# A two-block transformer kernel in split fp32: the closing layer norm moved to VectorE, and the last product's weights split during an earlier stage

## The chip, the cores and the metric

One core of one Trainium2 chip. The time is the device time of one execution in microseconds (us), median of three runs. The engines are called PE (TensorE), DVE (VectorE), ACT (ScalarE), POOL (GpSimd) and SP (SyncE, which issues the DMAs here).

## What is computed

Two blocks one after the other over 1024 tokens of width 1024, all in float32. The first has gated linear attention, a short convolution, a feed-forward part and a gated side input. The second has spatial gating, a convolution of 31 taps and attention in a window, whose three results are multiplied by `w_out_2`, added to the input and normed. The change touches the weights and the norm of the last two lines, and the feed-forward part's second product only as a place.

```python
h = h + (silu(a) * bb) @ w_down            # first block, feed-forward
...
def layer_norm(x, g, b):
    mu = jnp.mean(x, axis=-1, keepdims=True)
    var = jnp.mean(jnp.square(x - mu), axis=-1, keepdims=True)
    return (x - mu) * lax.rsqrt(var + 1e-5) * g + b
...
y = concatenate([ya, yb, yc], axis=-1) @ w_out_2      # second block
x = layer_norm(DEEPNORM_ALPHA * x + y, post_ln_g_2, post_ln_b_2)
```

## The kernel before

Every product runs on PE as three products of split operands: `split` (L308) makes a high part with an ACT copy (L313) and a low part with a DVE subtraction (L314), and `mm3` (L288) multiplies high by high, high by low and low by high (L293 to L295). Weights pass through one pool, `wts`: three raw tiles (raw0 to raw2), three of high and three of low parts; `load` (L85) fetches a tile, `split` (L104 ACT, L105 DVE) divides it.

The code is written as generators that are interleaved; a scheduler of the framework (`schedule_with_timeline_sim=True`) then fixes the order in which each engine gets its instructions. An engine works its queue in order, and SP issues all DMAs in order, so an instruction that waits holds up what is behind it on the same queue.

Three places matter here.

*The down projection* (`ffn_down`) multiplies the feed-forward's hidden values, which were spilled to DRAM as `sT`, by `w_down`. It runs in two parts of output columns; each part walks over pairs of hidden chunks. For each pair, `chunk` loads two pieces of `sT` (L987, tile sr) and splits them (tile s), one pair ahead of its 48 matmuls; a weight tile for the pair is loaded and split by the pool. This stage begins while the last of the up projection (`ffn_up`, L962 to L972) empties its banks.

*The attention units* of the second block (`run`): 16 units, one for each of 8 blocks of 128 tokens and 2 key heads. `att_scores` takes the scores (L1409 on PE, L1411 on DVE), the softmax (maximum L1414, exponentials L1418 and L1420 on ACT, sum L1421, reciprocal L1422, scaling L1426 on DVE and an ACT copy); `att_values` transposes, splits and multiplies by the values, and ends with L1455 (DVE) and L1456 (POOL) in the tile yc. During the first units `late_tiles` runs the last eight products of the block's input projection.

*The closing product.* With the fifth unit `finish_setup` loads the eight pieces of `w_out_2` (L1468, tile w2r) and splits each. Pieces 3 to 7 all use the raw tile raw0. From then on `finish(c)` runs for block c two blocks behind the attention: it loads the residual (L1489), splits ya and yb (low parts on POOL: mal) and yc, runs 48 matmuls (g), adds the residual on DVE (L1508), takes mean and variance (L1509, L1510), one over the root (L491 on DVE, L492 on POOL), and norms. For blocks 0 to 6 the norm is one small DVE product (L1513), an ACT pass (L1515: scale by the root's inverse, bias) and two POOL passes (L1516 by `post_ln_g_2`, L1517 plus `post_ln_b_2`); for block 7 it is two fused DVE instructions for each half of the columns (L1522, L1524). Then the result goes to DRAM (L1518, L1526).

Of the kernel before, what the change touches and what calls it, by code (L numbers as in the profile page):

```python
# [10 lines left out]
F32 = mybir.dt.float32  # L11
F32R = mybir.dt.float32r
U32 = mybir.dt.uint32
ACTF = mybir.ActivationFunctionType
ALU = mybir.AluOpType
# [4 lines left out]
D = 1024  # L20
# [115 lines left out]
class Kernel:  # L136
    def __init__(self, tc, ctx, I, out, dbg):
        self.tc, self.nc, self.ctx, self.I, self.out, self.dbg_out = tc, tc.nc, ctx, I, out, dbg or {}
        nc = self.nc
        self.cst = ctx.enter_context(tc.tile_pool(name="cst", bufs=1))  # L140
        self.wts = Weights(nc, ctx, tc, self.weight_plan())
        self.base = ctx.enter_context(tc.tile_pool(name="base", bufs=1))
        self.extra = None
        self.free_slots = {True: list(range(N_BASE)), False: []}
        self.slot_of = {}
        self.tmp = ctx.enter_context(tc.tile_pool(name="tmp", bufs=1))
        self.phase = None
        self.n_tmp = {}
        self.psum = self.banks = None
        self.dram = ctx.enter_context(tc.tile_pool(name="scr", bufs=1, space=DRAM))  # L150
        self.n_name = 0
        self.x_tiles = {}
        self.xT = self.dram.tile([2, 2, 128, 4, NH], F32, name="xT")
        self.hT = self.dram.tile([2, 2, 128, 4, NH], F32, name="hT")
        self.ppT = self.dram.tile([2, 128, 8, NH], F32, name="ppT")
        self.sT = self.dram.tile([NF, 128, 2, NH], F32, name="sT")


    def name(self, s):
# [818 lines left out]
    def ffn_down(self, N):  # L978

        nc, W = self.nc, self.wts  # L980
        kept = {}

        def chunk(k):
            if k in kept:
                return kept.pop(k)
            raw = self.temp([128, 2, NH], "sr", 2)
            nc.sync.dma_start(out=raw, in_=self.sT[k])  # L987
            s = self.slot([128, 4, NH], F32R, "s")
            self.split(s[:, 0:2, :], s[:, 2:4, :], raw)
            return s  # L990

        for hf in range(2):
            N[hf]["h"] = [self.slot([128, 4, NH], F32, "h", base=True) for _ in range(2)]
            for i in range(2):
                nc.sync.dma_start(out=N[hf]["h"][i], in_=self.hT[hf, i])
        self.stat = self.slot([128, 4, NH], F32, "stat", base=True)
        for hf in range(2):
            N[hf]["tiles"], N[hf]["act"] = [], []
        for part, pairs in enumerate(DOWN):
            ps = [self.psg("gx"[i // 4]) for i in range(8)]  # L1000
            nxt = [chunk(2 * pairs[0] + kk) for kk in range(2)]
            for n, j in enumerate(pairs):
                w = W.get("w_down", 256 * j, 2, part * 512, 512)
                s = nxt
                W.ahead()
                if n + 1 < len(pairs):
                    nxt = [chunk(2 * pairs[n + 1] + kk) for kk in range(2)]
                for half in range(2):
                    for kk in range(2):
                        for i in range(4 * half, 4 * half + 4):  # L1010
                            m, hf = divmod(i, 2)
                            wt = [x[:, kk, m * 128:(m + 1) * 128] for x in w]
                            self.mm3(ps[i], [(wt, (s[kk][:, hf, :], s[kk][:, 2 + hf, :]))],
                                     start=n == 0 and kk == 0, stop=n == len(pairs) - 1 and kk == 1)
                for kk in range(2):
                    if part == 0 and n >= len(pairs) - KEPT:
                        kept[2 * j + kk] = s[kk]
                    else:
                        self.release(s[kk])
            for hf in range(2):  # L1020
                tiles, act = self.alloc_act(4, True)
                N[hf]["tiles"] += tiles
                N[hf]["act"] += act
            for i in range(8):
                m, hf = divmod(i, 2)
                hm = N[hf]["h"][part][:, m, :]
                m += 4 * part
                nc.vector.tensor_tensor(out=hm, in0=ps[i], in1=hm, op=ALU.add)
                self.split(*N[hf]["act"][m], hm, self.v("ln3_g", m))
                self.square_acc(self.stat[:, hf, :], hm, m == 0)  # L1030
        for hf in range(2):
            N[hf]["r"] = self.norm_factor(hf, self.stat[:, hf, :])

    def load_pT(self):
        nc = self.nc
# [423 lines left out]
    def finish_setup(self):  # L1459
        nc, I = self.nc, self.I  # L1460
# [3 lines left out]
        nc.sync.dma_start(out=self.post[1], in_=I["post_ln_b_2"].to_broadcast([128, D]))  # L1464
        self.w2 = []
        for k in range(8):
            t = self.wts.pool.tile([128, D], F32, tag=f"raw{k if k < 3 else 0}", name=f"w2r{k}")
            nc.sync.dma_start(out=t, in_=I["w_out_2"][0, k * 128:(k + 1) * 128, :])  # L1468
            if k < 3:
                hi = self.wts.pool.tile([128, D], F32R, tag=f"hi{k}", name=f"w2h{k}")  # L1470
                lo = self.wts.pool.tile([128, D], F32R, tag=f"lo{k}", name=f"w2l{k}")
            elif k == 3:
                hi = self.wts.pool.tile([128, D], F32R, tag="raw1", name=f"w2h{k}")
                lo = self.wts.pool.tile([128, D], F32R, tag="raw2", name=f"w2l{k}")
            else:
                b = self.slot([128, 2, D], F32R, "w2")
                hi, lo = b[:, 0, :], b[:, 1, :]
            self.split(hi, lo, t)
            self.w2.append((hi, lo))

    def finish(self, c, ycs):

        nc = self.nc
        tok = slice(c * 128, (c + 1) * 128)
        if c % 2:
            res = self.wts.pool.tile([128, D], F32, tag="raw0", name=self.name("res"))
# [22 lines left out]
            nc.vector.bn_stats(out=st[:, 6 * n:6 * n + 6], in_=res[:, cl])  # L1509
        nc.vector.bn_aggr(out=st[:, 12:14], in_=st[:, 0:12])  # L1510
        self.small_rsqrt(st[:, 13:14], 1.0, 1e-5)
        if c < 7:
            nc.vector.tensor_scalar(out=st[:, 12:13], in0=st[:, 12:13], scalar1=st[:, 13:14], scalar2=-1.0, op0=ALU.mult,  # L1513
                                    op1=ALU.mult)
            nc.scalar.activation(out=res, in_=res, func=ACTF.Identity, scale=st[:, 13:14], bias=st[:, 12:13])  # L1515
            nc.gpsimd.tensor_tensor(out=res, in0=res, in1=self.post[0], op=ALU.mult)  # L1516
            nc.gpsimd.tensor_tensor(out=res, in0=res, in1=self.post[1], op=ALU.add)  # L1517
            nc.sync.dma_start(out=self.out[0, tok, :], in_=res)  # L1518
            return
        for n in range(2):  # L1520
            cl = slice(n * 512, (n + 1) * 512)
            nc.vector.scalar_tensor_tensor(out=res[:, cl], in0=res[:, cl], scalar=st[:, 12:13], in1=self.post[0][:, cl],  # L1522
                                           op0=ALU.subtract, op1=ALU.mult)
            nc.vector.scalar_tensor_tensor(out=res[:, cl], in0=res[:, cl], scalar=st[:, 13:14], in1=self.post[1][:, cl],  # L1524
# [119 lines left out]
```

## Time and profile before

| | |
|---|---|
| median of 3 runs | 1731.89 us (1731.1 to 1733.86) |
| profiled execution | 1733.28 us, its span 1731.5 us |
| PE clock granted, mean | 0.986 of full speed |
| PE busy | 1668.1 us (96% of the span) |
| DVE busy | 1135.5 us (66%) |
| ACT busy | 776.7 us (45%) |
| POOL busy | 377.6 us (22%) |
| DMA | 183.06 MB, mean 106 GB/s |

The busy times are of the whole span; the engines overlap, so they do not add up to it. The profile shows one execution on the hardware; the ends of matmuls in it are modelled. A line such as L1515 is a line of the kernel before. In the kernel after, lines behind L157 are higher by 1, those of `finish_setup` and what stands around it by 17 and less.

### The profile page before, as it was taken

The page shows a single profiled execution, that of the slowest core. Times are in us where ns is not written, and L with a number is a line of the kernel's source. Part 1 is how long each engine was busy: PE and PEld are TensorE (multiplying, and loading weights), DVE is VectorE, ACT ScalarE, POOL GpSimd, SP SyncE. Part 2 cuts the span into 40 slices and gives each one's busy share as a digit, 9 for nine tenths or more (in the row PEclk, how much of TensorE's full clock was granted, in tenths as well). Part 3 has the DMA queues.
Part 4 walks back from the last instruction along what each step waited for, and adds up shares of the span by engine and source line. Part 5 has one row for each costly group of instructions (what it writes and reads, how often), then busy time and mean ns, then how long its engine had stood idle before and what let it go on. Part 6 is the DMA issues. An engine that isn't in the chain of part 4 may idle for free.

```text
span 1731.5 us, 21021 instructions
## 1 busy us (share of the span) xinstructions
PE 1668.1 (96%) x7865; PEld 1380.5 (80%) x7865; DVE 1135.5 (66%) x1767; ACT 776.7 (45%) x1226; POOL 377.6 (22%) x307
## 2 busy tenths in 40 slices
PE   8999999999979999999999999999979999898997
PEld 6888987788758888888888888888858898786875
DVE  4256776987897556555644334329895998568786
ACT  5524246234555333333333223226577423578663
POOL 2010100200047444434420002003000000113664
PEclk9999999999999999999999999999989999999999
DMA  8233221324533222322236451434424412421111
GB/s 284 80 100 119 76 73 50 97 86 134 197 135 104 92 85 74 98 74 85 80 115 225 144 157 47 134 109 123 127 88 137 146 42 86 122 74 62 49 66 57
DMA packets 205022, 183.06 MB, mean 106 GB/s; under 512 B 8886, under 2 KB 173128, under 8 KB 203384
## 3 DMA queue, kind: packets, MB, share of 16 engines
q1 hardware_dynamic: 204920, 181.72, 33.4%
q8 instruction: 62, 1.02, 0.3%
q14 instruction: 40, 0.33, 0.1%
HBM read 149.17 MB, written 34.62 MB: 106 GB/s over the span
## 4 chain that ended last, share of the span: by engine, by line
PE 83%; DVE 9%; ACT 3%; issue 2%; DMA 2%; POOL 1%; SPq 0%; DVEq 0%; ACTq 0%; POOLq 0%
PE g L294 19%; PE g L295 19%; PE g L293 19%; PE x L293 6%; PE x L294 6%; PE x L295 6%; PE x L677 1%; DVE wl L105 1%; PE s L1409 1%; PE o L1447 1%; POOL sr L913 1%; PE t L1440 1%; PE x L639 1%; DVE stat L775 1%; DVE qpad L649 1%
## 5 line engine op out<-in xcount | busy, mean ns | idle before, releaser
L293 PE MATMUL g<-ah,wh 128*128 128x512 f32 x896 | 354.6, 399 | 11.4 <-issue 9.2
L294 PE MATMUL g<-al,wh 128*128 128x512 f32 x896 | 353.9, 396 | 0.4 <-DVE al L317 0.4
L295 PE MATMUL g<-ah,wl 128*128 128x512 f32 x896 | 353.8, 396 | 0.0
L104 ACT ACTIVATE wh<-wr 128x1024 fp32r<-128x1024 f32 (+1 forms) x142 | 150.2, 1061 | 267.3 <-PE g L294 170.1
L105 DVE TENSOR_TENSOR wl<-wr,wh 128x1024 fp32r<-128x1024 f32 (+1 forms) x142 | 181.1, 1278 | 117.6 <-ACT wh L104 113.8
L293 PEld LDWEIGHTS g<-ah,wh 128*128 128x128 f32 x896 | 169.7, 190 | 49.6 <-issue 11.6
L294 PEld LDWEIGHTS g<-al,wh 128*128 128x128 f32 x896 | 169.7, 189 | 37.9 <-issue 1.9
L295 PEld LDWEIGHTS g<-ah,wl 128*128 128x128 f32 x896 | 169.5, 189 | 37.3 <-issue 2.2
L314 DVE TENSOR_TENSOR s<-sr,s 128x1024 fp32r<-128x1024 f32 x36 | 44.0, 1222 | 99.9 <-ACT s L313 99.7
L913 POOL TENSOR_TENSOR sr<-wr,wr 128x512 f32<-128x512 f32 x22 | 46.5, 2112 | 180.2 <-DMA wr<-w_gate_upffn 143.0
L313 ACT ACTIVATE s<-sr 128x1024 fp32r<-128x1024 f32 x36 | 37.9, 1054 | 106.5 <-PE x L295 91.7
L958 POOL TENSOR_TENSOR t<-t,t 128x512 f32<-128x512 f32 x22 | 39.9, 1814 | 172.2 <-ACT t L941 172.2
L1299 DVE SCALAR_TENSOR_TENSOR cacc<-ypad,vec,cacc 128x1024 f32<-128x1024 f32 x60 | 76.1, 1292 | 0.4
L775 POOL TENSOR_TENSOR stat<-t,stat 128x512 f32<-128x512 f32 x14 | 23.5, 1703 | 234.6 <-ACT t L774 234.6
L293 PE MATMUL g<-s,wh 128*128 128x512 f32 x176 | 68.5, 389 | 0.0
L294 PE MATMUL g<-s,wh 128*128 128x512 f32 x176 | 68.5, 389 | 0.0
L295 PE MATMUL g<-s,wl 128*128 128x512 f32 x176 | 68.5, 389 | 0.0
L293 PE MATMUL x<-s,wh 128*128 128x512 f32 x176 | 68.5, 389 | 0.0
L294 PE MATMUL x<-s,wh 128*128 128x512 f32 x176 | 68.5, 389 | 0.0
L295 PE MATMUL x<-s,wl 128*128 128x512 f32 x176 | 68.5, 389 | 0.0
L649 DVE TENSOR_TENSOR qpad<-E,qk 64x64 f32<-64x64 f32 x224 | 51.2, 228 | 7.8 <-ACT E L641 5.0
L295 PE MATMUL g<-wh,al 128*128 128x256 f32 (+1 forms) x192 | 55.0, 288 | 0.0
(372 smaller groups left out, 3958.6 us busy)
## 6 DMA issues: line engine op xcount, KB each, us to landing
wr<-w_in SPq DMA_DIRECT2D x86, 512.0 KB
wr<-w_gate_upffn SPq DMA_DIRECT2D x44, 512.0 KB
sr<-sT SPq DMA_DIRECT2D x36, 512.0 KB
sT<-t SPq DMA_DIRECT2D x44, 256.0 KB
wr<-w_down SPq DMA_DIRECT2D x22, 512.0 KB
wr<-w_out SPq DMA_DIRECT2D x16, 512.0 KB
wr<-w_ple_gate SPq DMA_DIRECT2D x16, 512.0 KB
x<-x SPq DMA_DIRECT2D x8, 512.0 KB
```

What stands on the lines that cost most here:

```text
L104: self.nc.scalar.activation(out=hi[:, :n], in_=t[:, :n], func=ACTF.Copy)
L105: self.nc.vector.tensor_tensor(out=lo[:, :n], in0=t[:, :n], in1=hi[:, :n].bitcast(F32), op=ALU.subtract)
L293: mm(out=ps, lhsT=lh, rhs=rh, start=start and i == 0, stop=False)
L294: mm(out=ps, lhsT=lh, rhs=rl, start=False, stop=False)
L295: mm(out=ps, lhsT=ll, rhs=rh, start=False, stop=stop and i == n - 1)
L313: nc.scalar.activation(out=hi, in_=src, func=ACTF.Copy)
L314: (eng or nc.vector).tensor_tensor(out=lo, in0=src, in1=hi.bitcast(F32), op=ALU.subtract)
L649: nc.vector.tensor_tensor(out=qs[r, l, par, :].rearrange("p (b n) -> p b n", n=n), in0=right(E[r, 1 + l, :], n), in1=right(q[r], n), op=AL ...
L775: (eng or nc.gpsimd).tensor_tensor(out=acc, in0=sq, in1=acc, op=ALU.add)
L913: nc.gpsimd.tensor_tensor(out=t13[:, 0, :], in0=b12, in1=b11, op=ALU.subtract)
L958: nc.gpsimd.tensor_tensor(out=v5, in0=v5, in1=z7, op=ALU.add)
L1299: nc.vector.scalar_tensor_tensor(out=acc, in0=src, scalar=w, in1=acc, op0=ALU.mult, op1=ALU.add)
```

## The change

A DRAM tile `w2s` takes the split parts of `w_out_2`. A generator `split_w2` loads one piece of it into a tile w2r (two places), splits it into one of two tiles w2, and stores both parts; `ffn_down` takes one step of it in each pair of its first part, so eight steps in all. `finish_setup` no longer loads and splits: for each of the eight pieces it loads the two parts from `w2s`, 16 loads of 512 KB. In `finish` all blocks norm by the two fused DVE instructions: (res − mean) × `post_ln_g_2`, then × the root's inverse + `post_ln_b_2`; blocks 0 to 6 over the full width of 1024, block 7 in two halves as before. The ACT pass, the two POOL passes and the small DVE product are gone.

```diff
--- before.py
+++ after.py
@@ -154,6 +154,7 @@
         self.hT = self.dram.tile([2, 2, 128, 4, NH], F32, name="hT")
         self.ppT = self.dram.tile([2, 128, 8, NH], F32, name="ppT")
         self.sT = self.dram.tile([NF, 128, 2, NH], F32, name="sT")
+        self.w2s = self.dram.tile([8, 2, 128, D], F32, name="w2s")
 
 
     def name(self, s):
@@ -996,6 +997,7 @@
         self.stat = self.slot([128, 4, NH], F32, "stat", base=True)
         for hf in range(2):
             N[hf]["tiles"], N[hf]["act"] = [], []
+        early = self.split_w2()
         for part, pairs in enumerate(DOWN):
             ps = [self.psg("gx"[i // 4]) for i in range(8)]
             nxt = [chunk(2 * pairs[0] + kk) for kk in range(2)]
@@ -1005,6 +1007,7 @@
                 W.ahead()
                 if n + 1 < len(pairs):
                     nxt = [chunk(2 * pairs[n + 1] + kk) for kk in range(2)]
+                next(early, None)
                 for half in range(2):
                     for kk in range(2):
                         for i in range(4 * half, 4 * half + 4):
@@ -1030,6 +1033,20 @@
                 self.square_acc(self.stat[:, hf, :], hm, m == 0)
         for hf in range(2):
             N[hf]["r"] = self.norm_factor(hf, self.stat[:, hf, :])
+
+    def split_w2(self):
+
+        nc = self.nc
+        raw = self.slot([128, 2, D], F32, "w2r")
+        parts = [self.slot([128, 2, D], F32R, "w2") for _ in range(2)]
+        for k in range(8):
+            src, dst = raw[:, k % 2, :], parts[k % 2]
+            nc.sync.dma_start(out=src, in_=self.I["w_out_2"][0, k * 128:(k + 1) * 128, :])
+            self.split(dst[:, 0, :], dst[:, 1, :], src)
+            nc.sync.dma_start(out=self.w2s[k].rearrange("a p m -> p a m"), in_=dst.bitcast(F32))
+            if k == 7:
+                self.release(raw, *parts)
+            yield
 
     def load_pT(self):
         nc = self.nc
@@ -1464,8 +1481,6 @@
         nc.sync.dma_start(out=self.post[1], in_=I["post_ln_b_2"].to_broadcast([128, D]))
         self.w2 = []
         for k in range(8):
-            t = self.wts.pool.tile([128, D], F32, tag=f"raw{k if k < 3 else 0}", name=f"w2r{k}")
-            nc.sync.dma_start(out=t, in_=I["w_out_2"][0, k * 128:(k + 1) * 128, :])
             if k < 3:
                 hi = self.wts.pool.tile([128, D], F32R, tag=f"hi{k}", name=f"w2h{k}")
                 lo = self.wts.pool.tile([128, D], F32R, tag=f"lo{k}", name=f"w2l{k}")
@@ -1475,7 +1490,8 @@
             else:
                 b = self.slot([128, 2, D], F32R, "w2")
                 hi, lo = b[:, 0, :], b[:, 1, :]
-            self.split(hi, lo, t)
+            for i, t in enumerate((hi, lo)):
+                nc.sync.dma_start(out=t.bitcast(F32), in_=self.w2s[k, i])
             self.w2.append((hi, lo))
 
     def finish(self, c, ycs):
@@ -1509,16 +1525,7 @@
             nc.vector.bn_stats(out=st[:, 6 * n:6 * n + 6], in_=res[:, cl])
         nc.vector.bn_aggr(out=st[:, 12:14], in_=st[:, 0:12])
         self.small_rsqrt(st[:, 13:14], 1.0, 1e-5)
-        if c < 7:
-            nc.vector.tensor_scalar(out=st[:, 12:13], in0=st[:, 12:13], scalar1=st[:, 13:14], scalar2=-1.0, op0=ALU.mult,
-                                    op1=ALU.mult)
-            nc.scalar.activation(out=res, in_=res, func=ACTF.Identity, scale=st[:, 13:14], bias=st[:, 12:13])
-            nc.gpsimd.tensor_tensor(out=res, in0=res, in1=self.post[0], op=ALU.mult)
-            nc.gpsimd.tensor_tensor(out=res, in0=res, in1=self.post[1], op=ALU.add)
-            nc.sync.dma_start(out=self.out[0, tok, :], in_=res)
-            return
-        for n in range(2):
-            cl = slice(n * 512, (n + 1) * 512)
+        for cl in ([slice(0, 512), slice(512, 1024)] if c == 7 else [slice(0, 1024)]):
             nc.vector.scalar_tensor_tensor(out=res[:, cl], in0=res[:, cl], scalar=st[:, 12:13], in1=self.post[0][:, cl],
                                            op0=ALU.subtract, op1=ALU.mult)
             nc.vector.scalar_tensor_tensor(out=res[:, cl], in0=res[:, cl], scalar=st[:, 13:14], in1=self.post[1][:, cl],
```

The order of the engines is the same in both up to the start of the down projection, and again between there and the late products of the second block.

DVE at the start of the down projection, before. `t` are the last steps of the up projection, `s` the down projection's operands, `wl` a low part of `w_down`:

```order
661 L962 TENSOR_TENSOR t_6977<-x_6964,t_6977 128x512
662 L314 TENSOR_TENSOR s_7108<-sr_7106,s_7108 128x1024
663 L964 TENSOR_TENSOR t_6991<-x_6962,t_6977 128x512
664 L966 TENSOR_TENSOR t_7017<-t_7017,t_6977 128x512
665 L970 TENSOR_TENSOR t_6977<-x_6963,t_6977 128x512
666 L968 TENSOR_TENSOR t_7017<-t_7017,t_6991 128x512
667 L971 TENSOR_TENSOR t_6977<-t_6977,t_7019 128x512
668 L314 TENSOR_TENSOR s_7172<-sr_7170,s_7172 128x1024
669 L105 TENSOR_TENSOR wl_7229<-wr_7098,wh_7228 128x1024
```

The same place now; `w_797` and `w_798` are the low parts of the first two pieces of `w_out_2`, made from w2r:

```order
661 L963 TENSOR_TENSOR t_6978<-x_6965,t_6978 128x512
662 L315 TENSOR_TENSOR s_7109<-sr_7107,s_7109 128x1024
663 L965 TENSOR_TENSOR t_6992<-x_6963,t_6978 128x512
664 L967 TENSOR_TENSOR t_7018<-t_7018,t_6978 128x512
665 L315 TENSOR_TENSOR w_797_7118<-w2r_7117,w_797_7118 128x1024
666 L971 TENSOR_TENSOR t_6978<-x_6964,t_6978 128x512
667 L315 TENSOR_TENSOR w_798_7119<-w2r_7117,w_798_7119 128x1024
668 L969 TENSOR_TENSOR t_7018<-t_7018,t_6992 128x512
669 L972 TENSOR_TENSOR t_6978<-t_6978,t_7020 128x512
670 L315 TENSOR_TENSOR s_7180<-sr_7178,s_7180 128x1024
671 L105 TENSOR_TENSOR wl_7241<-wr_7099,wh_7240 128x1024
672 L315 TENSOR_TENSOR s_7185<-sr_7183,s_7185 128x1024
```

The two new subtractions stand between L967 and L971 and between L971 and L969; behind them two more follow in each of the next three pairs.

SP in the down projection, before, over two pairs:

```order
242 L987 DMA sr_7234<-sT 128x1024
243 L85 DMA wr_7232<-w_down 128x2x512
244 L987 DMA sr_7239<-sT 128x1024
245 L987 DMA sr_7298<-sT 128x1024
246 L85 DMA wr_7296<-w_down 128x2x512
247 L987 DMA sr_7303<-sT 128x1024
```

And now, behind the last store of the up projection:

```order
247 L988 DMA sr_7246<-sT 128x1024
248 L85 DMA wr_7244<-w_down 128x2x512
249 L988 DMA sr_7251<-sT 128x1024
250 L1046 DMA w2s<-w_797_7118 128x2x1024
251 L1044 DMA w2r_7117<-w_out 128x1024
252 L1046 DMA w2s<-w_798_7119 128x2x1024
253 L1044 DMA w2r_7117<-w_out 128x1024
254 L988 DMA sr_7314<-sT 128x1024
255 L85 DMA wr_7312<-w_down 128x2x512
256 L988 DMA sr_7319<-sT 128x1024
```

A store of both parts and the load of a next piece stand between the loads of the pair's own operands.

DVE in the tail where block 0's norm ends, before (`fst` holds mean and variance, `ast` and `sc` are the softmax's):

```order
1233 L1510 BN_AGGR fst_11924<-fst_11924 128x2
1234 L1426 TENSOR_SCALAR sc_11979<-sc_11979,ast_11978 128x384 x2
1235 L491 TENSOR_SCALAR fst_11924<-fst_11924 128x1
1236 L1455 TENSOR_TENSOR yc_12086<-o_12079,yc_12086 64x256
1237 L1421 TENSOR_TENSOR ast_12109<-ast_12109 128x4
1238 L1513 TENSOR_SCALAR fst_11924<-fst_11924 128x1
1239 L1422 RECIPROCAL ast_12109<-ast_12109 128x4
1240 L1426 TENSOR_SCALAR sc_12110<-sc_12110,ast_12109 128x384 x2
```

And now:

```order
1203 L1526 BN_AGGR fst_11944<-fst_11944 128x2
1204 L1433 TENSOR_TENSOR ast_11892<-sink_3665,ast_11892 128x4
1205 L492 TENSOR_SCALAR fst_11944<-fst_11944 128x1
1206 L1529 SCALAR_TENSOR_TENSOR res_11799<-res_11799,fst_11944,post_11768 128x1024
1207 L1531 SCALAR_TENSOR_TENSOR res_11799<-res_11799,fst_11944,post_11768 128x1024
1208 L1438 TENSOR_TENSOR ast_11892<-ast_11892 128x4
1209 L1439 RECIPROCAL ast_11892<-ast_11892 128x4
1210 L1443 TENSOR_SCALAR sc_11893<-sc_11893,ast_11892 128x384 x2
```

L1529 and L1531 are the fused instructions; L1438 and L1439 are L1421 and L1422 of before. The small product is gone, and the two passes over 1024 columns stand between the root and the softmax's sum.

## Rows read from the trace of the kernel before

**Rows 1.** The page's totals: busy us, share of the span, instructions.

```profile
PE 1668.1 (96%) x7865; PEld 1380.5 (80%) x7865; DVE 1135.5 (66%) x1767; ACT 776.7 (45%) x1226; POOL 377.6 (22%) x307
```

**Rows 2.** Table of stretches, down projection; columns in its first line.

```profile
core 0: us, PE busy (x) PEld busy (x) DVE busy (x) ACT busy (x) POOL busy (x), PEclk, DMA share, GB/s
930.00:940.00 10.00, 10.00 (x46) 8.29 (x45) 6.14 (x8) 2.29 (x4) 0.00 (x0) 1.00 0.94 372
960.00:970.00 10.00, 10.00 (x46) 8.28 (x45) 3.19 (x3) 2.19 (x3) 0.00 (x0) 1.00 0.47 150
```

**Rows 3.** Table of stretches, the tail; columns as in rows 2.

```profile
1570.00:1600.00 30.00, 24.12 (x111) 17.29 (x110) 27.28 (x72) 24.40 (x60) 11.55 (x15) 0.96 0.26 88
1600.00:1700.00 100.00, 95.77 (x469) 78.26 (x469) 76.84 (x200) 64.97 (x166) 58.29 (x57) 1.00 0.15 53
1660.00:1670.00 10.00, 8.70 (x44) 6.54 (x42) 8.60 (x20) 6.76 (x20) 8.11 (x10) 1.00 0.20 64
1680.00:1690.00 10.00, 7.50 (x42) 6.01 (x41) 8.17 (x22) 7.88 (x26) 6.54 (x7) 1.00 0.28 107
1700.00:1710.00 10.00, 6.63 (x24) 4.60 (x23) 7.42 (x12) 4.24 (x10) 5.18 (x5) 0.83 0.28 105
```

**Rows 4.** Chain of waits, 1590 to 1600: start us, us, what.

```profile
1591.63 3.23 DMA w2r<-w_out
...
1594.89 1.07 ACT w L313
```

**Rows 5.** Tile w2r: count, ns min/median/max, first and last start us.

```profile
L1468 SPq DMA_DIRECT2D w2r<-w_out x8: 327/328/341, 1529.3 to 1591.6; - x8
```

**Rows 6.** Groups, 1490 to 1732: count, busy us, mean ns, idle before.

```profile
L314 DVE TENSOR_TENSOR w<-w2r,w 128x1024 fp32r<-128x1024 f32 x4 | 5.0, 1239 | 1.3 <-ACT w L313 1.3
...
L313 ACT ACTIVATE w<-w2r 128x1024 fp32r<-128x1024 f32 x4 | 4.2, 1052 | 3.3 <-DMA w2r<-w_out 3.3
```

**Rows 7.** The same view: the closing norm's instructions.

```profile
L1516 POOL TENSOR_TENSOR res<-res,post 128x1024 f32<-128x1024 f32 x7 | 16.9, 2409 | 9.3 <-ACT res L1515 6.0 <-issue 2.3 <-POOL yc L1456 0.8
...
L1515 ACT ACTIVATE res<-res,fst 128x1024 f32<-128x1024 f32 x7 | 8.7, 1240 | 6.2 <-DVE fst L1513 6.2
...
L1513 DVE TENSOR_SCALAR fst<-fst 128x1 f32<-128x1 f32 x7 | 1.5, 213 | 1.6 <-POOL fst L492 1.5
...
L1522 DVE SCALAR_TENSOR_TENSOR res<-res,fst,post 128x512 f32<-128x512 f32 x2 | 1.4, 742 | 0.0
```

**Rows 8.** The page's groups over the whole span: the nearest operation.

```profile
L1299 DVE SCALAR_TENSOR_TENSOR cacc<-ypad,vec,cacc 128x1024 f32<-128x1024 f32 x60 | 76.1, 1292 | 0.4
```

**Rows 9.** Timeline of DVE, three of the seven stretched: start us, us, what.

```profile
1610.41 2.07 DVE L314 TENSOR_TENSOR mbl<-yc,mbh 128x256 fp32r<-128x256 f32 x1 [5.32 <-ACT mbh L313]
...
1645.48 2.36 DVE L1414 TENSOR_TENSOR ast<-ast,sink 128x4 f32<-128x4 f32 x1
...
1700.15 2.86 DVE L1426 TENSOR_SCALAR sc<-sc,ast 128x256 f32<-128x256 f32 x2
```

**Rows 10.** Timeline of POOL beside the second of them.

```profile
1645.23 2.59 POOL L1517 TENSOR_TENSOR res<-res,post 128x1024 f32<-128x1024 f32 x1
```

**Rows 11.** Line 1414 from 1570 on: ns min/median/max, first and last start.

```profile
L1414 DVE TENSOR_TENSOR ast<-ast,sink x11: 143/165/2360, 1572.9 to 1696.3; 128x4 f32<-128x4 f32 x11
```

**Rows 12.** Line 1421 from 1570 on: DVE idle before it until (us, times).

```profile
  ACT ast L1420: 7.7, 6
```

**Rows 13.** Groups, 930 to 1240: split of the down projection's operand.

```profile
L314 DVE TENSOR_TENSOR s<-sr,s 128x1024 fp32r<-128x1024 f32 x34 | 41.6, 1222 | 98.8 <-ACT s L313 98.8
```

**Rows 14.** Timeline of SP: two weight loads, one pair apart.

```profile
960.86 0.38 SPq L85 DMA_DIRECT2D wr<-w_down  x1
...
971.74 0.38 SPq L85 DMA_DIRECT2D wr<-w_down  x1
```

**Rows 15.** Timeline of DVE at the start of the down projection.

```profile
937.39 0.69 DVE L970 TENSOR_TENSOR t<-x,t 128x512 f32<-128x512 f32 x1
```

**Rows 16.** Timeline of PE: first product into the bank x.

```profile
942.22 0.39 PE L293 MATMUL x<-s,wh 128*128 128x512 f32 x1
```

## The prediction

> **What bounds the kernel now.** I read the page's totals first, then a table of stretches, and only there the waits. The totals [rows 1] say that TensorE (PE) is busy 96% of the span, so only time in which PE idles or runs at a lower clock can be won. The two stages that this change touches differ. In the down projection (930 to 970) PE has no gap while VectorE (DVE) falls to 32% and ScalarE (ACT) to 22% [rows 2]. In the tail from 1570 on, where the attention units of the second block and the closing product share PE, gaps appear: 24.12 us of work in 1570–1600, and 95.77 in 1600–1700 [rows 3]. So the question is what ends PE's waits in the tail, and whether the down projection has cover for what is put there.
>
> In 1590–1600 the chain of waits shows a load of the weights (3.23 us), ACT's split right behind it [rows 4], and then DVE's. The five rows k=3 to 7 share one raw buffer, so each load waits for the split before it. The last of the eight loads goes out at 1591.6 [rows 5], with attention long under way. In 1600–1700 PE's remaining gaps hang on DVE, ACT and POOL, none of which is full: 76.84, 64.97, 58.29 of 100.
>
> **Part 1: the weight splits leave the tail.** Removed there: 8 ACT copies (4 of them 4.2 us) and 8 DVE subtractions, 10.4 us (5.0 for the four shown, 5.4 for the four earlier ones) [rows 6]. In their place stand 16 loads of 512 KB. They carry 8.4 MB instead of 4.2 MB, on queues that are idle most of the time there (a DMA share of 0.26 and 0.15 [rows 3]). Loads for k=3 to 7 no longer wait for each other. PE idles 30.00 − 24.12 = 5.9 us in 1570–1600. I leave it the rate of the next stretch, 4.23 per 100, that is 1.3, and count 4.6 as won. Its granted clock there is 0.96: 0.04 × 24.12 = 1.0 us lost, of which the same share, 0.8, comes back. Sum **5.4**. The bounds are 0 (the attention's own waits take the place) and 6.9.
>
> **Part 2: the norm on DVE.** Removed for seven blocks: ACT's scale (8.7 us), two POOL passes (16.9 us for the one shown, 16.8 for L1517, together 33.7) and DVE's small product (1.5 us) [rows 7]. Added: 14 DVE instructions of 128x1024. The nearest row of that operation and shape takes 1292 ns [rows 8]; two halves as block 7 runs them take 2 × 742 = 1484 ns [rows 7], the upper bound. I take the first, since shape and operation are the same: 14 × 1.292 = **18.1 us** (20.8 at most).
>
> What DVE gets back is less visible. While POOL works on its long passes, a DVE instruction that begins inside one ends with it. DVE's L1414, a 128x4 operation that usually takes 165 ns, takes 2360 ns once: it starts at 1645.48 and ends at 1647.84; POOL's L1517 runs from 1645.23 to 1647.82 [rows 9, 10, 11]. Such stretched DVE instructions number seven, the first at 1610.41 and the last at 1700.15 [rows 9]; against their usual durations they lose 1.65 + 2.17 + 2.20 + 1.13 + 0.93 + 1.10 + 2.25 = **11.4 us**. They stand in the softmax, on the way to PE. They go with L1516 and L1517.
>
> So DVE gains 18.1 and loses 11.4 + 1.5. Where do the new instructions stand? In block 0's case directly ahead of the softmax's sum L1438 (L1421 before), the place where DVE now sits 7.7 us, in six waits, until ACT's exponentials are through [rows 12]. Of 18.1, 7.7 fit into that; 10.4 remain, against 12.9 that leave: **2.5** won. PE's gaps in the three worst stretches are 1.3 + 2.5 + 3.4 = 7.2 us, with a clock of 0.83 in the last, 0.17 × 6.63 = 1.1 us [rows 3]. The share 2.5 of 7.2 of that is 0.4. Sum **2.9**, bounds 0 and 8.3 (all gaps and all of the clock), and a loss in a rival below. ACT's 8.7 us and POOL's 33.7 I count as nothing: neither is full in any of these stretches except ACT in 1580–1590, whose load part 1 takes away. The last block keeps its halves, so the end of the kernel is untouched.
>
> **Part 3: the splits in the down projection.** Added beside PE: 8 ACT copies of 1.05 us [rows 6] and 8 DVE subtractions of 1.22 us (row of the same shape and stage [rows 13]), 8.4 and 9.8 us, on engines that are 22% and 32% busy [rows 2]; 8 loads (4.2 MB) and 8 stores (8.4 MB). The cover is PE's own work, which lasts longer than either. What can be late is a pair's own operands behind them: a pair lasts 971.74 − 960.86 = 10.88 us [rows 14], and in the order two k fall on most of the first pairs: 2 × 1.57 MB and the 1.57 MB of the pair's own make 4.7 MB. The queues moved 372 GB/s at a share of 0.94 [rows 2]: 4.7 MB are 12.7 us, 1.8 late per pair and some 7 after four pairs. An operand pair is loaded a pair ahead (10.88) and DVE and ACT have several us free behind the load; an estimate of the slack from these rows is 10 to 15 us. So I take **0**, with +5 as the bad end, and nothing below zero, since PE has no gap there to lose. The Trainium skill ("SBUF — State Buffer", the summary of rules for kernel authors) wants 358 GB/s for such transfers; the trace has shown 372 over 10 us, so the measurement decides. By the page 4.7 MB would take 13.1 us, 2.3 late per pair, with the same answer. SyncE issues all of these in order, so a store that waits for DVE's split holds up the loads behind it; DVE is idle two thirds of the time, so this wait is short.
>
> DVE's two first splits stand ahead of the last operations of the up projection, 2 × 1.22 = 2.4 us in front of L971 (L970 before, at 937.39). The bank that it empties is wanted by PE at 942.22 [rows 15, 16], so 942.22 − 938.1 = 4.1 us of slack cover them.
>
> **Sum.** 5.4 + 2.9 + 0 = 8.3 us. The profiled execution took 1733.28 us, its span 1731.5; the median of the three runs is 1731.89, 1.4 us lower. I set the sum against the median: 1731.9 − 8.3 = **1723.6 us**. Best case: 6.9 + 8.3 = 15.2, 1716.7.
>
> **Rivals.**
> (a) *The norm gives nothing back*: DVE's waits are merely filled elsewhere, and only part 1 counts: 1731.9 − 5.4 = 1726.5. For it: part 2 nets only 2.5 us of DVE.
> (b) *The weights were not the bound*: gaps in 1570–1600 come back as waits of the softmax, and only part 2 counts: 1729.0. For it: ACT and DVE have 24.40 and 27.28 of 30 us there [rows 3], part of it attention. Against it: the chain of waits goes through the weights.
> (c) *The down projection pays*: PE waits there for late operands or the queue, 5 us of part 3's bad end: 1728.6. Against it: 10 us and more of slack.
> (d) *DVE becomes the bound of the tail* (slower). Its place is the DVE queue in 1600–1700. With six blocks there, 6 × 2 × 1.29 = 15.5 us come on 76.84: 92.3 of 100, if the stretched instructions do not leave, because the new ones have both inputs in SBUF and stall with the POOL work that stays. DVE idles 23.2 us of the 100 now. If three quarters of that (17.4) are waits that nothing in its queue's order can fill, the stretch needs 92.3 + 17.4 = 109.7; over seven blocks instead of six 9.7 × 7/6 = 11.3 us more, less 5.4 of part 1: 1737.8. It comes out slower than before where 12.3 of the 23.2 us cannot be filled. Against it: the new instructions stand in one of these waits, and seven long POOL passes a stage are gone.
> The Trainium skill ("SBUF — State Buffer", who interferes with whom) says that a DVE instruction with two SBUF inputs and a GpSimd one that reads SBUF exclude each other for their whole length, which speaks for (d). The trace agrees on the exclusion: 2360 ns instead of 165 [rows 9, 11].
> That the change does not do what it says has no chance: in the order the splits are gone from the tail and the two fused instructions stand in each block.
>
> **How the numbers follow.** Forecast 0.50; (a) 0.18; (b) 0.10; (c) 0.09; (d) 0.13. 0.2% of this kernel, 3.5 us, is about what a measurement can tell from no change. Forecast and (a) are faster: 0.68. (b) and (c) lie within 3.5 us: 0.19. (d) is slower: 0.13. The range leaves out (d): from the best case, rounded to **1716**, up to (b) and (c) with the other part at its worse end and the 1.4 us between profiled run and median, **1733**.
>
> **What would show it.** Right: in 1570–1600 PE is busy over 28 us of 30 and no chain there goes through weights; no 128x4 DVE instruction of over 1 us in 1600–1700; the new DVE instructions at 1.25 to 1.5 us; PE without a gap from 930 to 1030. Wrong: gaps of PE in the first five pairs of the down projection; the new instructions at 2 us and more beside POOL's; waits of PE or ACT for DVE that grow in 1600–1700 with DVE over 90 of 100; or gaps in 1570–1600 that end on the softmax.

## The result, and the profile after

The changed kernel takes 1713.67 us (median of 4 runs, 1713.18 to 1716.37), the kernel before beside it 1732.22. That is 18.6 us faster by the medians, where 8.3 were forecast, and below the range, which began at 1716. The ratio is 0.9888, 95% interval 0.9875 to 0.9901, which is 19.4 us of 1732; the experiments below are compared by ratios. The profiled execution has 1713.7 us, its span 1711.7. Line numbers below are those of the changed kernel unless said otherwise: L1431 is L1414 of before, L1438 is L1421, L1443 is L1426, L1426 is L1409, L1428 is L1411.

The page's totals after, which answer to [rows 1]:

```profile
span 1711.7 us, 21055 instructions
...
PE 1660.5 (97%) x7865; PEld 1379.6 (81%) x7865; DVE 1139.7 (67%) x1774; ACT 768.0 (45%) x1219; POOL 347.4 (20%) x293
```

PE's 7865 matmuls are the same. Its busy time fell from 1668.1 to 1660.5, by 7.6 us, and its idle time from 1731.5 − 1668.1 = 63.4 to 1711.7 − 1660.5 = 51.2, by 12.2. Together these are the 19.8 us of the two spans. All of it lies behind 1570: from there to the end it was 161.5 us and is 141.7 now.

The table of stretches after (columns as in [rows 2]); the first two lines cover the down projection, as [rows 2] do, and the others answer to [rows 3]:

```profile
860.00:1240.00 380.00, 380.00 (x1673) 313.56 (x1672) 195.64 (x212) 146.69 (x184) 39.61 (x28) 1.00 0.47 164
930.00:940.00 10.00, 10.00 (x46) 8.29 (x45) 5.96 (x8) 3.71 (x4) 0.00 (x0) 1.00 1.02 419
1570.00:1600.00 30.00, 29.55 (x147) 24.56 (x146) 23.90 (x66) 22.23 (x61) 12.06 (x16) 1.00 0.20 75
1600.00:1700.00 100.00, 98.46 (x490) 81.42 (x489) 89.79 (x221) 60.71 (x166) 44.39 (x50) 1.00 0.16 59
1660.00:1670.00 10.00, 10.00 (x49) 8.18 (x48) 9.77 (x26) 5.81 (x18) 5.28 (x6) 1.00 0.28 97
1680.00:1690.00 10.00, 10.00 (x49) 8.17 (x48) 9.38 (x19) 6.23 (x19) 6.21 (x6) 1.00 0.26 101
```

In the down projection PE has no gap, with the DMA queues at a share of 1.02 in 930–940. In 1570–1600 it works 29.55 us instead of 24.12, in 1600–1700 98.46 instead of 95.77, while DVE went from 76.84 to 89.79. Closer windows of before show where the clock was low, two places of 10 us, and the 5 us ahead of the first:

```profile
1590.00:1595.00 5.00, 3.66 (x16) 2.45 (x15) 5.00 (x13) 1.66 (x5) 1.16 (x2) 1.00 0.31 107
1595.00:1600.00 5.00, 3.91 (x11) 2.76 (x11) 4.40 (x13) 4.90 (x14) 2.06 (x4) 0.74 0.33 104
1600.00:1605.00 5.00, 5.00 (x21) 4.00 (x21) 4.68 (x18) 4.95 (x15) 1.72 (x3) 0.92 0.02 4
1700.00:1705.00 5.00, 2.41 (x11) 1.61 (x9) 4.63 (x6) 2.16 (x6) 3.06 (x3) 0.82 0.26 105
1705.00:1710.00 5.00, 4.22 (x15) 2.99 (x15) 2.79 (x6) 2.08 (x5) 2.12 (x3) 0.84 0.30 105
```

At both places PE had stood still (3.66 us of work in 1590–1595, 2.41 in 1700–1705). The means 0.74 to 0.92 are mixtures of the two levels, 1.2 and 2.4 GHz; the share lost is 0.26 + 0.08 + 0.18 + 0.16 of 5 us each, 3.4 us, and that is an upper bound, as PE did not work through all of these 20 us. After the change PEclk is 1.00, the level of 2.4 GHz, in 1570–1600 and in 1600–1700. PE's named waits from 1570 to the end (us in total, times, longest), before:

```profile
PE s L1409 <- DVE ast L1411: 4.1, 4, 2.5
PE g L293 <- ACT w L313: 2.1, 2, 1.6
PE g L294 <- DVE w L314: 1.6, 3, 0.5
...
```

And after, all of them:

```profile
PE s L1426 <- DVE ast L1428: 1.5, 1, 1.5
PE g L294 <- ACT mbh L314: 0.8, 2, 0.4
```

The long pauses of DVE's small instructions are gone too. L1414 of before took up to 2360 ns [rows 11]; now (ns min/median/max):

```profile
L1431 DVE TENSOR_TENSOR ast<-ast,sink x10: 143/298/716, 1584.3 to 1679.6; 128x4 f32<-128x4 f32 x10
```

### The profile page after: what moved, and what is told of

It reads as the page before. It is cut to its first block, busy times and chain, and to the rows that moved or that the text cites. A ratio compares the mean times of both kernels' runs of the same rounds, so it can differ in the third digit from the quotient of the medians.

```text
span 1711.7 us, 21055 instructions
## 1 busy us (share of the span) xinstructions
PE 1660.5 (97%) x7865; PEld 1379.6 (81%) x7865; DVE 1139.7 (67%) x1774; ACT 768.0 (45%) x1219; POOL 347.4 (20%) x293
## 3 DMA queue, kind: packets, MB, share of 16 engines
q8 instruction: 62, 1.02, 0.2%
## 4 chain that ended last, share of the span: by engine, by line
PE 88%; DVE 7%; ACT 2%; issue 1%; DMA 1%; POOL 0%; SPq 0%; DVEq 0%; ACTq 0%; POOLq 0%
PE g L295 20%; PE g L294 20%; PE g L296 20%; PE x L294 6%; PE x L296 6%; PE x L295 6%; PE x L678 1%; PE s L1426 1%; PE t L1457 1%; PE o L1464 1%; PE x L640 1%; DVE wl L105 1%; DVE qpad L650 1%; PE x L366 1%; PE x L700 0%
## 5 line engine op out<-in xcount | busy, mean ns | idle before, releaser
L294 PE MATMUL g<-ah,wh 128*128 128x512 f32 x896 | 354.2, 399 | 11.3 <-issue 8.8
```

The costliest lines, as they stand in the source:

```text
L294: mm(out=ps, lhsT=lh, rhs=rh, start=start and i == 0, stop=False)
```

## The experiments

All ratios are against the kernel before on the same chip. The scheduler writes a new order for every kernel, so each run changes the order as well as what is named.

| run | splits in the tail | norm of blocks 0 to 6 | ratio (95%) |
|---|---|---|---|
| before | yes | ACT, two POOL passes | 1 |
| e1_weights_only | no | ACT, two POOL passes | 1.0011 (0.9999 to 1.0022) |
| e2_norm_only | yes | DVE | 0.9946 (0.9930 to 0.9961) |
| e3_no_pool_passes | yes | ACT alone | 0.9958 (0.9944 to 0.9973) |
| the change | no | DVE | 0.9888 (0.9875 to 0.9901) |
| e4_no_norm | no | none | 0.9883 (0.9861 to 0.9906) |
| e7_weights_no_pool | no | ACT alone | 0.9911 (0.9895 to 0.9926) |
| e8_pool_passes_back | no | DVE, then two POOL passes | 0.9992 (0.9982 to 1.0001) |
| e9_quarter_passes | no | DVE, then eight short POOL passes | 0.9976 (0.9963 to 0.9989) |
| e10_pool_writes | no | DVE, then five POOL writes | 0.9918 (0.9890 to 0.9945) |
| e5_two_raw | yes, two raw buffers | ACT, two POOL passes | 0.9997 (0.9986 to 1.0008) |
| e6_two_raw_norm | yes, two raw buffers | DVE | 0.9953 (0.9935 to 0.9970) |
| e11_idle_splits | yes, unread | DVE | 0.9966 (0.9955 to 0.9977) |

**The parts alone.** e1 is the changed kernel with the old end of `finish`:

```diff
-        for cl in ([slice(0, 512), slice(512, 1024)] if c == 7 else [slice(0, 1024)]):
+        if c < 7:
...
+            nc.scalar.activation(out=res, in_=res, func=ACTF.Identity, scale=st[:, 13:14], bias=st[:, 12:13])
+            nc.gpsimd.tensor_tensor(out=res, in0=res, in1=self.post[0], op=ALU.mult)
+            nc.gpsimd.tensor_tensor(out=res, in0=res, in1=self.post[1], op=ALU.add)
```

> Only the weights' part of the change; the norm of blocks 0 to 6 stays on ACT and POOL. Theory (each part clears its own stretch, gaps and low clock together): about 9 us faster than before, near 1723; the stretch around 1570 to 1600 loses its gaps of 5.9 us and its low clock, those behind 1650 stay. Rival (the softmax's waits take the weights' place, as the forecast half assumed): 5 us or less. Second rival (the two parts need each other): nearly no gain.

The second rival held: 1736.2 us, no gain. The stretches of e1:

```profile
1570.00:1600.00 30.00, 28.42 (x145) 23.36 (x143) 21.37 (x59) 20.79 (x57) 14.41 (x17) 1.00 0.18 74
1600.00:1650.00 50.00, 45.48 (x196) 35.65 (x197) 39.99 (x97) 29.39 (x72) 26.36 (x27) 0.90 0.17 63
1650.00:1700.00 50.00, 45.20 (x220) 36.73 (x219) 43.08 (x110) 34.43 (x93) 24.48 (x26) 0.97 0.12 43
```

and of the kernel before, 1600 to 1700:

```profile
1600.00:1650.00 50.00, 49.56 (x242) 40.76 (x241) 38.65 (x96) 32.48 (x82) 31.31 (x30) 0.99 0.15 53
1650.00:1700.00 50.00, 46.21 (x229) 37.50 (x229) 38.19 (x105) 32.48 (x85) 26.98 (x27) 1.00 0.15 54
```

Most of the gaps of 1570–1600 are gone (28.42 of 30), as the first theory had it. But in 1600–1650, where the kernel before has 0.4 us of gaps, 4.5 us stand now, with a clock of 0.90 and 196 matmuls instead of 242. DVE in e1, an instruction of 128x4 at 1640.27:

```profile
1640.27 2.83 DVE L1438 TENSOR_TENSOR ast<-ast 128x4 f32<-128x4 f32 x1 [0.41 <-ACT ast L1437]
```

and POOL beside it:

```profile
1640.73 2.34 POOL L1533 TENSOR_TENSOR res<-res,post 128x1024 f32<-128x1024 f32 x1
```

They end together, at 1643.10 and 1643.07. My reading, not tested by itself: before, PE came to the first POOL pass at 1606 with closing products in arrears and worked on them while the softmax was held up; without the splits it has no such stock, and each hold is a gap.

e2 is the kernel before with the new end of `finish`, the reverse of the diff above.

> Only the norm's part of the change; the eight weight splits stay in the tail. Theory: about 9 us faster, near 1723; the gaps of 7.2 us in 1660 to 1710 go whole, with the low clock at 1700, though DVE does 18 us more. Rival (the forecast's balance of DVE time, 2.5 us net): 3 us faster. Second rival (DVE too full with the splits and the norm): no gain or slower.

The theory held: 1724.51 us, 9.4 us by the ratio (0.54% of 1732). The gaps stay in 1570–1600 and go behind it:

```profile
1570.00:1600.00 30.00, 25.05 (x116) 18.15 (x115) 27.46 (x69) 23.68 (x58) 11.50 (x14) 0.94 0.21 71
1600.00:1650.00 50.00, 50.00 (x249) 41.81 (x248) 43.75 (x105) 32.27 (x89) 22.09 (x25) 1.00 0.21 74
1650.00:1700.00 50.00, 49.19 (x245) 39.62 (x244) 43.21 (x114) 32.13 (x89) 21.82 (x24) 1.00 0.15 54
```

The parts are therefore not a sum: nothing and 9.4 alone, 19.4 together, all by the ratios.

**Is it POOL's passes or DVE's time?** e3 is the kernel before without the passes:

```diff
-            nc.gpsimd.tensor_tensor(out=res, in0=res, in1=self.post[0], op=ALU.mult)
-            nc.gpsimd.tensor_tensor(out=res, in0=res, in1=self.post[1], op=ALU.add)
```

> The kernel before without POOL's two long passes of blocks 0 to 6 (scale by and addition of the closing norm's vectors are left out there), so DVE is freed of stretched instructions and gets no new work. Theory (the stretched DVE instructions cause the gaps behind 1600): as fast as the norm on DVE alone, within 2 us. Rival (DVE time counts, and the 18 us on DVE cost something): 5 us or more faster than the norm on DVE alone. Second rival (POOL's passes do not matter): within 2 us of before.

1726.35 us, 1.8 above e2, which has all of the norm on DVE: the theory held, and the norm on DVE cost nothing there that could be seen. (e3 still has ACT's pass and the small DVE product, so e4 below is the cleaner case.) e7 leaves the same two lines out of e1.

> The weights' part, and POOL's two long passes of blocks 0 to 6 left out (no scale by and addition of the closing norm's vectors there); ACT's pass stays, DVE gets nothing new. Theory (POOL's passes keep the weights' part from paying): near the kernel after, 1712 to 1716, some 20 us faster than the weights' part alone. Rival (the order that the scheduler wrote for the weights' part alone is at fault): 1725 or more.

1717.57 us: 1.00% or 17.3 us better than e1, by the passes alone. It misses the upper end of the theory's 1716 by 1.6, far from the rival. By the ratios e3 is 2.1 us behind e2 and e7 4.0 behind the change; ACT's pass, which e3 and e7 keep, may cost something, but the intervals overlap, so that is not shown. e4 takes the fused instructions of blocks 0 to 6 out of the changed kernel.

```diff
+        if c < 7:
+            nc.sync.dma_start(out=self.out[0, tok, :], in_=res)
+            return
```

> The kernel after with the two fused DVE instructions of blocks 0 to 6 left out (their rows go out without the closing norm's scale and bias). Theory (the 18 us that the norm adds to DVE lie in DVE's own waits and cost nothing): within 3 us of the kernel after, near 1713. Rival (the forecast: DVE time beyond 7.7 us counts, 10 us of it): 6 us or more faster, near 1705.

1712.4 us, 0.05% or 0.9 us below the change, inside its interval: the theory held. The intervals leave room for a cost of some 5 us, but not for the 10 of the rival. DVE's groups from 1570 on (count, busy us, mean ns, idle before), without the norm:

```profile
L315 DVE TENSOR_TENSOR mbl<-yc,mbh 128x256 fp32r<-128x256 f32 x15 | 7.1, 471 | 10.2 <-ACT mbh L314 10.0
...
L1438 DVE TENSOR_TENSOR ast<-ast 128x4 f32<-128x4 f32 x11 | 1.9, 176 | 11.3 <-ACT ast L1437 11.2
```

and after the change:

```profile
L1529 DVE SCALAR_TENSOR_TENSOR res<-res,fst,post 128x1024 f32<-128x1024 f32 x7 | 10.0, 1429 | 0.0
L1531 DVE SCALAR_TENSOR_TENSOR res<-res,fst,post 128x1024 f32<-128x1024 f32 x7 | 9.4, 1348 | 0.7 <-POOL fst L493 0.6
...
L315 DVE TENSOR_TENSOR mbl<-yc,mbh 128x256 fp32r<-128x256 f32 x15 | 7.0, 466 | 3.5 <-ACT mbh L314 3.4
...
L1438 DVE TENSOR_TENSOR ast<-ast 128x4 f32<-128x4 f32 x11 | 2.7, 248 | 2.6 <-ACT ast L1437 2.5
```

The waits ahead of L1438 and of the closing product's low part went from 11.3 + 10.2 to 2.6 + 3.5: of the 10.0 + 9.4 = 19.4 us that the norm of blocks 0 to 6 takes on DVE, 15.4 lie in these two. e8 puts POOL passes back into the changed kernel:

```diff
+            if c < 7:
+                nc.gpsimd.tensor_tensor(out=res, in0=res, in1=self.post[0], op=ALU.add)
+                nc.gpsimd.tensor_tensor(out=res, in0=res, in1=self.post[0], op=ALU.subtract)
```

> The kernel after with two POOL passes of 128x1024 put behind the norm of blocks 0 to 6 (they add the scale vector and subtract it again). Nothing of the softmax reads what they write. Theory (a long POOL pass holds DVE's two-input instructions for its length, whoever waits for the pass): 15 us slower than the kernel after or more, 1728 to 1740. Rival (what cost time was the way of the norm over ACT and POOL, or the splits): within 4 us of the kernel after.

1733.09 us: 1.04%, 18.0 us, is lost again, though nothing but the result's DMA waits for these passes. The passes, and DVE's softmax scaling beside them (ns min/median/max):

```profile
L1534 POOL TENSOR_TENSOR res<-res,post 128x1024 f32<-128x1024 f32 x7 | 17.3, 2471 | 3.0 <-DVE ast L1438 1.4 <-DVE res L1531 1.4
...
L1535 POOL TENSOR_TENSOR res<-res,post 128x1024 f32<-128x1024 f32 x7 | 16.7, 2386 | 0.4
```

```profile
L1443 DVE TENSOR_SCALAR sc<-sc,ast x22: 333/420/2560, 1576.1 to 1700.3; 128x384 f32<-128x384 f32 x18, 128x256 f32<-128x256 f32 x4
```

**How do the passes hurt?** e9 cuts each pass of e8 into four (the first of the two is shown):

```diff
-                nc.gpsimd.tensor_tensor(out=res, in0=res, in1=self.post[0], op=ALU.add)
+                for q in range(4):
+                    ql = slice(q * 256, (q + 1) * 256)
+                    nc.gpsimd.tensor_tensor(out=res[:, ql], in0=res[:, ql], in1=self.post[0][:, ql], op=ALU.add)
```

> The kernel after with the same two POOL passes behind the norm of blocks 0 to 6 as in e8_pool_passes_back, each in four instructions of 128x256. The same work on POOL and nearly the same time, but no instruction longer than about 0.8 us. Theory (what hurts is the length for which one POOL instruction holds DVE): half of the 19 us or more comes back, 1714 to 1723. Rival (the total of POOL's time beside DVE is what counts): still 1728 or more.

1730.57 us: the theory fell. By the ratios only 2.8 of the 18.0 us come back, and the intervals of e8 and e9 overlap. The pieces take 41 us in all instead of 34, and they run back to back (idle before them, in all: 0.2 and 4.3 us):

```profile
L1539 POOL TENSOR_TENSOR res<-res,post 128x256 f32<-128x256 f32 x28 | 21.1, 777 | 0.2
L1536 POOL TENSOR_TENSOR res<-res,post 128x256 f32<-128x256 f32 x28 | 20.0, 747 | 4.3 <-DVE ast L1438 1.4 <-DVE ast L1433 1.4 <-issue 1.2
```

Four such pieces in a row can hold a DVE instruction of 128x4 as long as the whole pass did. POOL's row, and DVE's:

```profile
1694.51 2.76 POOL L1539 TENSOR_TENSOR res<-res,post 128x256 f32<-128x256 f32 x4
...
1694.82 2.48 DVE L1438 TENSOR_TENSOR ast<-ast 128x4 f32<-128x4 f32 x1
```

They end together, at 1697.27 and 1697.30. Most holds of e9 are shorter, up to about 1 us. So cutting a pass into pieces that follow each other at once does not shorten every hold, and e9 does not rule out that the length of a hold counts. Pieces with room between them were not tried.

e10 writes a constant instead:

```diff
+            if c < 7:
+                for _ in range(5):
+                    nc.gpsimd.memset(res, 0.0)
```

> The kernel after with five POOL writes of a constant to 128x1024 behind the norm of blocks 0 to 6 in the place of the passes of e8_pool_passes_back (the rows of those blocks go out as zeros). POOL is taken for about the same 4.8 us a block, but reads nothing. Theory (DVE and POOL exclude each other over reading): within 4 us of the kernel after, 1713 to 1718, and no stretched DVE instruction. Rival (POOL's own queue is late with the attention's small steps): as e8_pool_passes_back, 1728 or more.

1722.11 us, between the two: by the ratios 5.2 us above the change (the intervals overlap) and 12.8 below e8. POOL was taken as long as in e8:

```profile
L1535 POOL MEMSET res<- 128x1024 f32 x35 | 33.5, 958 | 4.2 <-DVE res L1531 2.8
```

L1431, a DVE instruction with two inputs from SBUF, is no longer held for long; its 696 ns are no more than the 716 after the change (ns min/median/max):

```profile
L1431 DVE TENSOR_TENSOR ast<-ast,sink x11: 142/163/696, 1570.2 to 1685.4; 128x4 f32<-128x4 f32 x11
```

but the tensor_scalar L1443, with one, is held more than after the change, where its median is 410 and its longest 898:

```profile
L1443 DVE TENSOR_SCALAR sc<-sc,ast x22: 360/662/1716, 1574.9 to 1693.1; 128x384 f32<-128x384 f32 x18, 128x256 f32<-128x256 f32 x4
```

and PE now waits most for yc's high part, which ACT makes once POOL's own small multiplication in yc is done (ACT idles 5.2 us for that, 3.8 after the change; us, times, longest):

```profile
PE g L294 <- ACT mbh L314: 4.8, 4, 2.6
```

So most of the damage goes with the reading. "No stretched instruction" was wrong for tensor_scalar. Whether the remaining 5.2 us are more than noise is not shown, nor how they would split between the held tensor_scalars and POOL's late queue.

**What do the splits cost?** e5 is the kernel before with another raw buffer for two pieces, e6 the same with the norm of e2:

```diff
+            if k in (4, 6):
+                t = self.temp([128, D], "res", 1)
+            else:
...
```

> The kernel before with the raw pieces 4 and 6 of the closing weights in a second buffer (that of the even blocks' residual), so that their loads no longer wait for the split before; the eight splits stay. Theory (the chain of load and split through one buffer is what makes PE wait in 1570 to 1600): 4 to 8 us faster, most of what the weights' part gives. Rival (the ACT and DVE time of the splits is what counts): within 2 us of before.

> Both norm on DVE and the second raw buffer for pieces 4 and 6; the eight splits stay in the tail, nothing is kept in DRAM. Theory (the load chain through one buffer is what the weights' part removes, and it shows once POOL's passes are gone): near the kernel after, 1713 to 1717. Rival (the splits' ACT and DVE time counts too): near the norm alone, 1721 to 1725.

1733.61 us against 1733.50 before, and 1724.56 against e2's 1724.51: the rival held both times. The gaps move, they don't go. e5:

```profile
1570.00:1600.00 30.00, 28.48 (x135) 22.45 (x134) 25.75 (x71) 23.51 (x59) 9.75 (x13) 1.00 0.22 71
1600.00:1700.00 100.00, 89.44 (x428) 73.03 (x427) 82.17 (x201) 64.05 (x166) 56.34 (x54) 0.95 0.15 53
```

and e6:

```profile
1570.00:1600.00 30.00, 28.46 (x142) 22.67 (x141) 26.72 (x68) 22.97 (x60) 12.23 (x15) 1.00 0.21 73
1600.00:1650.00 50.00, 47.43 (x234) 39.07 (x234) 44.41 (x112) 33.71 (x90) 22.18 (x25) 0.97 0.15 54
```

In e5 the stretch 1570–1600 is as full as in e1, which has no splits there, and 10.6 us of gaps stand in 1600–1700 instead of 4.2. In e6 2.6 us of them stand in 1600–1650, which e2 fills. PE waits for no weight from 1570 on in either run, against 3.7 us before (2.1 + 1.6), so the load chain had its part in the gaps of that stretch, but taking it away alone pays nothing. e11 gives the changed kernel splits that nobody waits for:

```diff
+        for k in range(8):
+            hi = self.wts.pool.tile([128, D], F32R, tag="raw0", name=f"dh{k}")
+            lo = self.temp([128, D], "res", 1, F32R)
+            self.split(hi, lo, self.w2[k][0].bitcast(F32))
```

> The kernel after with eight more splits (ACT copy and DVE subtraction of 128x1024) of the loaded weights in the tail, into tiles that nobody reads. No weight waits for them. Theory (what the weights' part removes, once the norm is on DVE, is the ACT and DVE time of the splits ahead of the attention): as slow as the norm alone, 1720 to 1726. Rival (it removes PE's wait for late weights, and the engines' time costs nothing, as with the norm): within 3 us of the kernel after.

1728.71 us, 0.78% or 13.5 us above the change: on the theory's side, but 2.7 above its range. No matmul waits for a weight from 1570 on, but the gaps and the low clock of 1570–1600 are back:

```profile
1570.00:1600.00 30.00, 25.49 (x120) 20.58 (x118) 26.73 (x66) 26.82 (x62) 14.07 (x13) 0.89 0.31 120
1600.00:1700.00 100.00, 96.32 (x471) 77.81 (x472) 87.12 (x227) 64.25 (x173) 43.74 (x49) 1.00 0.16 57
```

with PE waiting for the attention's scores and probabilities:

```profile
PE s L1426 <- DVE ast L1428: 3.9, 3, 2.2
PE o L1464 <- ACT t L314: 1.6, 3, 0.9
```

e11 does more than take time on ACT and DVE. Its unread tiles lie in the residual's buffers, so the residual's load of blocks 0 and 1 waits for them until 1597, and the closing product's first addition comes as late as before. That addition (ns min/median/max, first and last start) before, after the change, in e6 and in e11:

```profile
L1508 DVE TENSOR_TENSOR res<-g,res x16: 672/684/692, 1598.5 to 1723.8; 128x512 f32<-128x512 f32 x16
L1524 DVE TENSOR_TENSOR res<-g,res x16: 653/681/692, 1582.7 to 1704.0; 128x512 f32<-128x512 f32 x16
L1511 DVE TENSOR_TENSOR res<-g,res x16: 670/675/692, 1588.0 to 1713.3; 128x512 f32<-128x512 f32 x16
L1528 DVE TENSOR_TENSOR res<-g,res x16: 672/676/692, 1600.4 to 1720.9; 128x512 f32<-128x512 f32 x16
```

So e11 alone does not separate the splits' time from a late start of the closing product. e6 starts only 5.3 us later than the change and waits for no weight, and is still 11.3 us slower by the ratios, which speaks for the splits' time. How much each counts, and which of the two engines, is open.

## Why the prediction was wrong

**The direction was right, and so was the mechanism of part 2, POOL's holds; the sum was not.** What was named to be seen was seen: PE over 28 us in 1570–1600, no 128x4 DVE instruction over 1 us, no gap in the down projection. The fused instructions took 1.43 and 1.35 us on average, inside the 1.25 to 1.5 that were named, the longest 1.76.

- **The first failed step is "of 18.1, 7.7 fit into that; 10.4 remain".** I weighed DVE time gained against DVE time lost, and so counted only 2.5 us of 12.9. The new instructions took 19.4 us and cost 0.9, inside the noise (e4), since DVE also waits for ACT ahead of the closing product's low part; and the gaps were not made by DVE's total but by POOL's holds of its small instructions (e3, e8). The part alone is worth 9.4 us instead of 2.9 (e2).
- **The second is the sum itself, 5.4 + 2.9.** The weights' part is worth nothing with POOL's passes (e1), and without them 8.1 us (e3 to e7, 0.9958 − 0.9911) to 10.0 (e2 to the change, 0.9946 − 0.9888). I took the stretches 1570–1600 and 1600–1700 for independent; a gap that goes from one comes back in the other as long as something there still holds the attention, as POOL's passes do in e1. That is the mechanism of rival (b), and e1 shows it.
- **Part 1's 5.4 was priced on the wrong thing.** I read PE's wait for the weights out of the chain [rows 4, 5]. Row and wait were true: with the chain loosened the stretch 1570–1600 fills up (e5, e6). But the time does not fall, so what the weights' part pays is not that wait. e6 and e11 point to the ACT and DVE time of the splits ahead of the attention; a part of the late start of the closing product is not excluded. A wait that ends last is not what its removal gives.
- **The remaining gaps and PE's busy time were mis-sized, which put the time outside the range.** I left 1.3 us in 1570–1600 and most of 7.2 behind; after the change 0.45 and 1.54 (of 1600–1700) are left. Idle time fell by 12.2 us, not by 4.6 + 2.5, and PE's busy time by 7.6, not by 0.8 + 0.4. Of the latter at most 3.4 are the clock by the closer windows; what the rest is stays open. The best case of 1716.7 held 13.1 us of gaps, more than went, but for PE's busy time only the clock's 1.0 + 1.1, so the range ended too high.
- **The zero for the down projection was right**: PE is without a gap there, and the queues moved 419 GB/s in 930–940 where I had reckoned with 372.
- Rival (d) asked for waits of DVE that nothing can fill: it needed 12.3 us of them in 1600–1700, and DVE is now idle only 10.2 there, with PE at 98.46. Of (a) and (b), which each let one part count alone, (a) had it the wrong way round: it is the norm that pays alone, and the weights' part that does not.

## What to carry to other kernels

Where PE is nearly full, ask of an engine's work what it holds up and where it stands, not how much it is: 19 us of new work in DVE's waits cost nothing that could be seen, eight splits ahead of the attention (about 10 us of DVE) cost 8 to 10, and 34 us on a half idle POOL cost 18. Two causes of gaps that follow each other in a pipeline are not to be added: removing the first can pay nothing until the second goes, so price each with and without the other. GpSimd work that reads SBUF beside VectorE's small steps has a price even if nobody waits for its result.

## What the runs showed of the hardware

The Trainium skill ("SBUF — State Buffer", who interferes with whom) says that a DVE instruction with two SBUF inputs contends with GpSimd work that reads SBUF but not with work that only writes it. It also says that a tensor_scalar can enter a two-port mode, in which it contends with GpSimd. The trace agrees: beside POOL's writes the two-input L1431 took at most 696 ns, the tensor_scalar L1443 up to 1716 ns, where its longest after the change was 898; which mode L1443 ran in no run here shows.

The hold goes both ways. After the change POOL's one-column step of the root, a median of 0.55 us before, takes longer where it starts inside a fused DVE instruction (ns min/median/max):

```profile
L493 POOL TENSOR_TENSOR fst<-fst,mhalf x8: 552/1458/1526, 1587.7 to 1706.0; 128x1 f32<-128x1 f32 x8
```

The first of them runs from 1587.71 to 1589.17, behind L1529 (1587.49 to 1588.77), and L1531 waits 0.45 us for it.

I had not expected that short POOL instructions give so little back: cut into quarters of 0.75 us, the same passes still cost 15.2 us of 18.0.
